# A two-layer trunk in fp32 on one core: the last four row blocks of layer 1's down projection as Strassen block products, and the second feed-forward group's weights prepared before the first group is evacuated

## The chip, the core and the metric

The kernel runs on one core of a Trainium2 chip. A core has five engines, each with its own list of instructions that it works through in order: TensorE (PE in the profile; PEld is its loading of weights), VectorE (DVE), ScalarE (ACT), GpSimd (POOL) and SyncE (SP, which here only issues DMAs). They meet through semaphores. The metric is the time of one execution in microseconds (us) on the device; less is better.

## The reference

Input x is 512 tokens by 1024, in fp32. Two layers follow, each with a mixer and a gated feed-forward part, then a last RMS norm:

```python
def gated_conv_ffn(x, w_gate, w_up, conv_w, conv_b, w_down):
    g = jnp.einsum('bsd,df->bsf', x, w_gate)            # 1024 -> 2816
    g = causal_dwconv3(g, conv_w) + conv_b
    up = jnp.einsum('bsd,df->bsf', x, w_up)             # 1024 -> 2816
    return jnp.einsum('bsf,fd->bsd', jax.nn.silu(g) * up, w_down)   # 2816 -> 1024

for layer in range(2):
    xn = rms_norm(h, norm_mix[layer])
    h = h + mixer(xn)          # layer 0: gated conv and pooling; layer 1: chunked spatial gating
    hn = rms_norm(h, norm_ffn[layer])
    h = h + gated_conv_ffn(hn, ...)
return rms_norm(h, final_norm)
```

## The kernel before

**Precision.** Every fp32 matrix is split into a high and a low part (`whi`/`wlo` for weights, `a_hi`/`a_lo` and `hgh`/`hgl` for activations), and a product is three matmuls: high by high, high by low, low by high (`mm3`, lines 154 to 156; `multiply`, line 543). There are two ways to make the parts of a weight tile. `parts` (L146) copies the high part on ScalarE (L149) and subtracts on VectorE (L150). `summed` (L136) writes the negated high part into `lo` on ScalarE (L140), has a GpSimd DMA add the raw weights to it (L141), and copies the high part (L143).

**Feed-forward.** The 2816 hidden columns are 22 row blocks of 128. They are worked in groups of two blocks: group 0 directly (`direct`), groups 2, 4, ..., 20 in `both` by Strassen's scheme (seven products instead of eight) for gate and up together, 14 products of twelve matmuls of 256 columns. `both(f)` first fetches and combines the weights: the unit a11, the sums s12 and s34 for gate and up (L691 to 719), then runs the products and evacuates them: ScalarE copies banks out (L733), VectorE adds and applies the convolution taps (`conv`, L575 and L577), ScalarE the SiLU (L585). Group 0 is evacuated by the function that `direct` returns (L619 to 631): VectorE scales the gate banks (L624), taps, SiLU, multiplication with the up banks (L630). There are seven PSUM banks for all this.

**Down projection.** `steps` runs the groups in the order of STEPS; after a group comes a part of the down projection of earlier blocks (`half_down`, in layer 1 four row blocks for one half of the 1024 columns). What is left at the end is `last_down` for blocks 18 to 21: eight pieces of 128 tokens by 512 columns, each twelve matmuls (the last piece in two halves of 256 columns). `done` adds a piece to the residual y (L1100), sums its squares (L1145), multiplies by the final gain into `yf` (L1148) and, when a row of 1024 is complete, takes the root (L1158), finishes the norm on VectorE in the columns up to 672 (L1163) and on ScalarE in the rest (L1167), and stores (L1168, L1169). Before it, `root` (L1122) is a one-element square root of a constant that is ready at the very start.

**Order.** A scheduler puts each engine's instructions into a fixed order when the kernel is built, from the order in which the code emits them and what they depend on; `behind` and `inorder` pin a few. Tiles come from pools with a set number of buffers (`raw` 4, `whi` and `wlo` 6 each, `sum` 3, `c` 2); an instruction that writes a tile waits until the buffer's last user is done. Each engine then keeps its order: what stands behind a waiting instruction waits too.

Of the kernel before, what the change touches and what calls it, by code (L numbers as in the profile page):

```python
# [8 lines left out]
F32 = mybir.dt.float32  # L9
# [3 lines left out]
ALU = mybir.AluOpType  # L13
PSUM = bass.MemoryType.PSUM

P = 128
# [16 lines left out]
def tile_trunk(ctx: ExitStack, tc: tile.TileContext, x, norm_mix, norm_ffn, final_norm,  # L33
# [520 lines left out]
    class Ffn:  # L554
# [127 lines left out]
        def both(self, f):  # L682
# [12 lines left out]
            for key in "gu":  # L695
# [23 lines left out]
                put(key, 3, w, 1)  # L719

            banks = {"g": {}, "u": {}}
# [44 lines left out]
        def hidden(self, f, before=lambda i, j: None):  # L766

            if f == 0:
# [11 lines left out]
                rows = rest()  # L780
            else:
                rows = self.both(f)
            return rows
# [293 lines left out]
    def ffn1(norm):  # L1077
        with tc.tile_pool(name="f1", bufs=1) as ap:
# [39 lines left out]
            def last_down(a, b):  # L1118
                fin = wp.tile([P, D], F32, tag="raw", bufs=4, name="fin")
                nc.scalar.dma_start(  # L1120
                    fin, final_norm.rearrange("(o d) -> o d", o=1).to_broadcast([P, D]))
# [7 lines left out]
                def lhs(ft, piece):  # L1129
                    ts_ = slice(piece[0] * P, (piece[0] + 1) * P)  # L1130
                    return acts[ft][0][:, ts_], acts[ft][1][:, ts_]

                def rhs(ft, piece):
                    c = slice(*piece[1:])
                    return ch[ft][0][:, 0, c], ch[ft][1][:, 0, c]

                yf = {}

                def done(piece, ps):
                    t, c0, c1 = piece  # L1140
                    dst = y[t][:, c0:c1]
                    add(dst, ps, t)
                    sq = tp.tile([P, S], F32, tag="sq", name=f"sqf{t}_{c0}")[:, : c1 - c0]
                    ss = ssf[:, t, c0 // 256 : c0 // 256 + 1]
                    nc.scalar.activation(sq, dst, AF.Square, accum_out=ss)  # L1145
                    if c0 == 0:
                        yf["row"] = ap.tile([P, D], F32, tag="sum", bufs=3, name=f"yf{t}")
                    nc.vector.tensor_tensor(yf["row"][:, c0:c1], dst, fin[:, c0:c1], ALU.mult)  # L1148
                    ms = ssf[:, t, 0:1]
                    if c0 == 0:  # L1150
                        nc.vector.tensor_scalar(ss, ss, 1.0 / D, EPS, op0=ALU.mult, op1=ALU.add)
                        return
                    nc.vector.scalar_tensor_tensor(ms, ss, 1.0 / D, ms, op0=ALU.mult, op1=ALU.add)
                    if c1 < D:
                        return
                    r = tp.tile([P, LINE], F32, tag="rc", name=f"rc_fin{t}")[:, :1]
                    sd = work("sd", 1, f"fin{t}")
                    nc.scalar.activation(sd, ms, AF.Sqrt)  # L1158
                    nc.vector.reciprocal(r, sd)
                    nc.vector.scalar_tensor_tensor(ms, ms, r, r, op0=ALU.mult, op1=ALU.mult)  # L1160
                    nc.vector.tensor_scalar(ms, ms, -0.5, 1.5, op0=ALU.mult, op1=ALU.add)
                    lo, hi = slice(0, SHARE), slice(SHARE, D)
                    nc.vector.tensor_scalar(y[t][:, lo], yf["row"][:, lo], r, ms, op0=ALU.mult,  # L1163
                                            op1=ALU.mult)
                    both = ssf[:, t, 1:2]
# [55 lines left out]
```

## Time and profile before

| | us |
|---|---|
| median of 3 runs (991.19 to 992.14) | 991.21 |
| the profiled execution | 991.47 |
| its span | 989.4 |
| TensorE busy | 978.7 |
| VectorE busy | 770.3 |
| ScalarE busy | 549.6 |
| GpSimd busy | 101.0 |

TensorE's clock was granted at full speed throughout (0.999). A row of the timeline has the start in us, the duration in us, the engine, the line, the operation, the tiles written and read, and in brackets how long the engine stood idle before it and what ended that. A row for a stretch has its bounds, its length, then for PE, PEld, DVE, ACT and POOL the busy time and the number of instructions, the granted clock, the DMA engines' share and GB/s. A row of waits has who waited for whom, the total in us, how often, and the longest. A row of DMA issues ends with the median us from issue to landing.

### The profile page before, as it was taken

How to read it: one execution, taken by the hardware profiler on the slowest of the kernel's cores; microseconds unless marked ns; L12 is line 12 of the kernel's file. 1: busy time of each engine (PE TensorE's matmuls, PEld its weight loads, DVE VectorE, ACT ScalarE, POOL GpSimd, SP SyncE). 2: the span in 40 equal slices, each digit the busy share in tenths (PEclk: the TensorE clock that was granted, in tenths of full speed). 3: DMA queues.
4: the chain of work that ended last, by engine and by line, in shares of the span. 5: the costliest groups of instructions: out<-in, count | busy, mean ns of one | idle time of the engine just before them, and what ended most of it. 6: DMA issues, size and time to landing. Idle time of an engine off the chain costs nothing.

```text
span 989.4 us, 15461 instructions
## 1 busy us (share of the span) xinstructions
PE 978.7 (99%) x6117; PEld 882.7 (89%) x6117; DVE 770.3 (78%) x1170; ACT 549.6 (56%) x823; POOL 101.0 (10%) x118
## 2 busy tenths in 40 slices
PE   9999999999999999999999999999999999999997
PEld 6788888899999999999889988889999999999986
DVE  5897458998788887886887665589987779777776
ACT  5623346765465654655487734676655456554544
POOL 2142022100000000000210001210000000000000
PEclk9999999999999999999999999999999999999999
DMA  7342225555455454553324623265555555455512
GB/s 247 131 149 85 86 86 128 131 143 153 129 149 133 131 142 129 150 129 110 124 64 116 199 74 102 54 139 129 150 162 134 131 148 146 118 136 135 143 49 85
DMA packets 86420, 125.64 MB, mean 127 GB/s; under 512 B 4196, under 2 KB 58188, under 8 KB 86348
## 3 DMA queue, kind: packets, MB, share of 16 engines
q1 hardware_dynamic: 77228, 98.24, 32.1%
q0 software_dynamic: 7200, 24.12, 13.4%
q10 hardware_dynamic: 1920, 2.30, 0.8%
q8 instruction: 48, 0.79, 0.3%
q14 instruction: 24, 0.20, 0.1%
HBM read 98.42 MB, written 2.10 MB: 102 GB/s over the span
## 4 chain that ended last, share of the span: by engine, by line
PE 85%; DVE 6%; ACT 3%; issue 1%; DMA 0%; ACTq 0%; POOL 0%; DVEq 0%
PE dn L154 4%; PE dn L155 4%; PE dn L156 4%; PE d L155 3%; PE d L154 3%; PE d L156 3%; PE oo L156 1%; PE oo L154 1%; PE oo L155 1%; PE oe L156 1%; PE oe L155 1%; PE oe L154 1%; PE u_20a L543 1%; PE u_18a L543 1%; PE u_16a L543 1%
## 5 line engine op out<-in xcount | busy, mean ns | idle before, releaser
L154 PE MATMUL dn<-whi_dn,a_hi 128*128 128x512 f32 (+1 forms) x180 | 69.3, 385 | 0.0
L155 PE MATMUL dn<-wlo_dn,a_hi 128*128 128x512 f32 (+1 forms) x180 | 69.3, 385 | 0.0
L156 PE MATMUL dn<-whi_dn,a_lo 128*128 128x512 f32 (+1 forms) x180 | 69.2, 384 | 0.0
L577 DVE SCALAR_TENSOR_TENSOR c<-rows,prm,c 128x512 f32<-128x512 f32 x88 | 63.8, 746 | 0.2 <-ACT c L575 0.2
L141 POOL DMA_DIRECT2D wlo_g<-raw_g x20 | 17.2, 861 | 385.2 <-ACT wlo_g L140 369.6
L154 PE MATMUL d<-a_hi,whi_d 128*128 128x512 f32 x144 | 56.1, 390 | 0.0
L155 PE MATMUL d<-a_lo,whi_d 128*128 128x512 f32 x144 | 56.1, 390 | 0.0
L156 PE MATMUL d<-a_hi,wlo_d 128*128 128x512 f32 x144 | 56.0, 389 | 0.0
L150 DVE TENSOR_TENSOR wlo_dn<-raw_dn,whi_dn 128x1024 fp32r<-128x1024 f32 x22 | 26.9, 1224 | 26.2 <-ACT whi_dn L149 26.0
L680 DVE TENSOR_TENSOR wlo_s34u<-s34u,whi_s34u 128x1024 fp32r<-128x1024 f32 x20 | 24.5, 1225 | 26.7 <-ACT whi_s34u L679 26.7
L1100 DVE SCALAR_TENSOR_TENSOR y<-dn,small,y 128x512 f32<-128x512 f32 (+1 forms) x49 | 33.9, 737 | 8.8 <-PE dn L156 8.8
L156 PEld LDWEIGHTS dn<-whi_dn,a_lo 128*128 128x128 f32 x180 | 33.8, 188 | 6.9 <-DVE a_lo L263 0.2
L154 PEld LDWEIGHTS dn<-whi_dn,a_hi 128*128 128x128 f32 x180 | 33.9, 188 | 6.5
L155 PEld LDWEIGHTS dn<-wlo_dn,a_hi 128*128 128x128 f32 x180 | 33.9, 188 | 6.3
L143 ACT ACTIVATE whi_u<-raw_u 128x1024 fp32r<-128x1024 f32 x21 | 22.1, 1055 | 30.0 <-PE d L155 16.3
L149 ACT ACTIVATE whi_dn<-raw_dn 128x1024 fp32r<-128x1024 f32 x22 | 23.3, 1059 | 25.5 <-issue 12.6
L261 ACT ACTIVATE a_hi<-s 128x512 fp32r<-128x512 f32 x44 | 27.4, 625 | 18.0 <-PE dn L155 12.3
L150 DVE TENSOR_TENSOR wlo_d<-raw_d,whi_d 128x1024 fp32r<-128x1024 f32 x18 | 22.0, 1224 | 19.7 <-ACT whi_d L149 19.7
L199 ACT ACTIVATE hgh<-h,prm 128x512 fp32r<-128x512 f32 x24 | 17.3, 723 | 35.1 <-DVE h L310 35.0
L585 ACT ACTIVATE s<-c,prm 128x512 f32<-128x512 f32 x44 | 31.2, 714 | 9.3 <-DVE c L577 9.3
L141 POOL DMA_DIRECT2D wlo_u<-raw_u x21 | 18.1, 862 | 166.4 <-ACT wlo_u L140 83.8
L210 POOL TENSOR_TENSOR ssq_f<-ssq_f,sq_f 128x512 f32<-128x512 f32 x14 | 19.8, 1412 | 131.2 <-ACT sq_f L209 96.3
(1435 smaller groups left out, 3664.0 us busy)
## 6 DMA issues: line engine op xcount, KB each, us to landing
raw_g<-in_w_ffn_gate_dram SPq DMA_DIRECT2D x40, 512.0 KB, 3.9
raw_u<-in_w_ffn_up_dram SPq DMA_DIRECT2D x40, 512.0 KB, 3.7
raw_dn<-in_w_ffn_down_dram SPq DMA_DIRECT2D x22, 512.0 KB, 3.6
wlo_u<-raw_u POOLq DMA_DIRECT2D x21, 512.0 KB, 5.6
wlo_g<-raw_g POOLq DMA_DIRECT2D x20, 512.0 KB, 4.7
raw_d<-in_w_ffn_down_dram SPq DMA_DIRECT2D x18, 512.0 KB, 3.7
raw_oe<-in_w_out_even_dram SPq DMA_DIRECT2D x8, 512.0 KB, 3.6
raw_v<-in_w_in_odd_dram SPq DMA_DIRECT2D x8, 512.0 KB, 4.6
```

The source lines that it names most:

```text
L141: nc.gpsimd.dma_start(lo, raw, accum_op=ALU.add)
L149: behind(nc.scalar.activation(hi, raw, AF.Copy), after[1])
L150: behind(nc.vector.tensor_tensor(lo, raw, hi.bitcast(F32), ALU.subtract), after[0])
L154: nc.tensor.matmul(ps, lhs[0], rhs[0], start=start, stop=False)
L155: nc.tensor.matmul(ps, lhs[0], rhs[1], start=False, stop=False)
L156: nc.tensor.matmul(ps, lhs[1], rhs[0], start=False, stop=stop)
L261: nc.scalar.activation(hi, src, AF.Copy, scale=scale)
L543: nc.tensor.matmul(ps, l, r, start=first, stop=end, skip_group_check=True)
L577: nc.vector.scalar_tensor_tensor(c, t[:, i : S + i], prm("cf", i * NF + ft), c, op0=ALU.mult, op1=ALU.add)
L585: nc.scalar.activation(s, c, AF.Silu, bias=self.prm("bf", ft))
L680: nc.vector.tensor_tensor(lo, src, hi.bitcast(F32), ALU.subtract)
L1100: nc.vector.scalar_tensor_tensor(dst, ps, ffn.cols[:, t : t + 1], dst, op0=ALU.mult, op1=ALU.add)
```

## The change

**Group 2.** `both` is cut in two, `prepare` (fetch and combine weights) and `products`. In group 0, `prepare(2)` is now called before the returned evacuation `rest()`, so group 2's weights are emitted ahead of it. This is in both layers.

**The last part of layer 1's down projection.** Blocks 18 to 21 (two by two) times 1024 columns (two halves) for 512 tokens (two halves) become seven Strassen products, each for two token tiles. The four weight blocks are fetched and combined by four subtractions (`less`), and all seven weight operands are split by `summed`, so their low parts come by GpSimd's DMA instead of VectorE. The activations are combined on VectorE and split into the tiles of `hg` (`block`) instead of being split row by row. Products accumulate in shared banks, each partial sum being added to y as it stands (`add`); `finish` does what `done` did, with the gain multiplication on GpSimd for the first two token tiles. `fin` moves from the `raw` pool to `sum`, the finished rows from `sum` to `raw`. The one-element square root `root` is gone.

```diff
-        def both(self, f):
+        def prepare(self, f):
...
+            return stat
+
+        def products(self, f, stat):
...
-                rows = rest()
-            else:
-                rows = self.both(f)
-            return rows
+                self.second = self.prepare(2)
+                return rest()
+            return self.products(f, self.second if f == 2 else self.prepare(f))
...
-            def last_down(a, b):
-                fin = wp.tile([P, D], F32, tag="raw", bufs=4, name="fin")
...
-                root = small[:, 2:3]
-                nc.scalar.activation(root, eps, AF.Sqrt)
-                ch = {}
-                for ft in range(a, b):
-                    ch[ft] = weights(w_ffn_down[1][ft * P : (ft + 1) * P, :]
-                                     .rearrange("(k p) c -> p k c", p=P), 1, D, f"dn1_{ft}")
...
+            def finish(t, c0, c1, ssums={}):
+                dst = y[t][:, c0:c1]
+                sq = tp.tile([P, S], F32, tag="sq", name=f"sqf{t}_{c0}")[:, : c1 - c0]
+                ss = ssf[:, t, c0 // 256 : c0 // 256 + 1]
+                nc.scalar.activation(sq, dst, AF.Square, accum_out=ss)
+                if t not in ssums:
+                    row = wp.tile([P, D], F32, tag="raw", bufs=4, name=f"yf{t}")
+                    ssums[t] = [ss, row, 0]
+                ms, row, seen = ssums[t]
+                times = nc.gpsimd if t < 2 else nc.vector
+                times.tensor_tensor(row[:, c0:c1], dst, fin[:, c0:c1], ALU.mult)
...
+                share = SHARE if t == NT - 1 else S
+                lo, hi = slice(0, share), slice(share, D)
...
+            a = NF - 4
+            rows = {ft: row for ft, row in ffn.steps(half_down, before)}
+            raw = {(i, j): fetch(
...
+                for i, j in ((0, 0), (0, 1), (1, 1), (1, 0))}
+            fin = ap.tile([P, D], F32, tag="sum", bufs=3, name="fin")
...
+            less(t1, b12, b11)
+            put(1, summed, b11)
+            put(2, summed, b21)
+            less(t2, b22, t1)
+            put(5, summed, t1)
+            put(6, summed, t2)
+            less(b12, b22, b12)
+            put(3, summed, b22)
+            put(7, summed, b12)
+            less(b21, b21, t2)
+            put(4, summed, b21)
...
+            block(1, 0, a11)
+            block(2, 1, a12)
+            for n in range(2):
+                nc.vector.tensor_tensor(s1[:, n], a21[n], a22[n], ALU.add)
+            block(5, 4, s1)
+            for n in range(2):
+                nc.vector.tensor_tensor(s2[:, n], s1[:, n], a11[n], ALU.subtract)
+            block(6, 5, s2)
+            for n in range(2):
+                nc.vector.tensor_tensor(a12[n], a12[n], s2[:, n], ALU.subtract)
+            block(3, 6, a12)
+            for n in range(2):
+                nc.vector.tensor_tensor(a21[n], a11[n], a21[n], ALU.subtract)
+            block(7, 2, a21)
+            block(4, 3, a22)
...
+            for i in range(2):
+                add(y[i][:, left], product(1, i), i)
+            for i in range(2):
+                add(y[i][:, left], product(2, i), i)
+                finish(i, 0, 512)
+            for i in range(2):
+                add(y[2 + i][:, right], product(5, i), 2 + i)
+            for i in range(2):
+                add(y[i][:, right], product(6, i), i)
+            for i in range(2):
+                add(y[i][:, right], product(3, i), i)
+                finish(i, 512, D)
+            for i in range(2):
+                add(y[2 + i][:, right], product(7, i), 2 + i)
+                finish(2 + i, 512, D)
+
+            add(y[3][:, 256:512], banks["a", 1][:, 256:512], 3)
+            for i, c0, c1, bank in ((0, 0, 512, None), (1, 0, 256, None), (1, 256, 512, "c")):
+                add(y[2 + i][:, c0:c1], product(4, i, c0, c1, bank), 2 + i)
+                finish(2 + i, c0, c1)
```

`put` calls `summed` for a product's weight operand; `product(p, i, ...)` issues the twelve matmuls' half of a product, six for token tile i of 128 rows, with the weights as the moving side. The product 4 of the second tile is done in two pieces of 256 columns.

More of the change, by code (lines that the diff above doesn't have):

```diff
@@ new lines, in ffn1, with put, less @@
+            b11, b12, b21, b22 = (raw[at][0] for at in ((0, 0), (0, 1), (1, 0), (1, 1)))
+            t1, t2 = (ap.tile([P, 2, S], F32, tag="sum", bufs=3, name=f"dnt{i}") for i in (1, 2))
+            stat = {}
+            def put(product, how, src):
+                stat[product] = how(src, 2, 512, f"dnp{product}")
+            def less(dst, x, y_):
+                behind(nc.vector.tensor_tensor(dst, x, y_, ALU.subtract), ffn.added["u"])
+            less(t1, b12, b11)
+            put(1, summed, b11)
@@ new lines, in ffn1 @@
+            left, right = slice(0, 512), slice(512, D)
+            for i in range(2):
[10 more added lines that the diff above has]
+                finish(i, 512, D)
```

104 lines of the change are left out of this document (53 added, 51 removed).

## The prediction

> **What bounds the kernel now.** I read the page's busy shares first, then TensorE's waits, then the stretches where it waited, then the first 40 us and the end by engine.
>
> ```profile
> PE 978.7 (99%) x6117; PEld 882.7 (89%) x6117; DVE 770.3 (78%) x1170; ACT 549.6 (56%) x823; POOL 101.0 (10%) x118
> ...
> q0 software_dynamic: 7200, 24.12, 13.4%
> ...
> wlo_u<-raw_u POOLq DMA_DIRECT2D x21, 512.0 KB, 5.6
> ```
>
> ```profile
> PE u_2e L543 <- DVE wlo_s12u L680: 1.9, 2, 0.9
> ...
> PE g_2a L543 <- ACT rows L733: 0.2, 1, 0.2
> ```
>
> TensorE is the bound: what is taken from its list is worth its own time, unless another engine is then last. It stands still only in group 2 of each layer, at the start, and at the end. The next view is busy time in the two stretches from the first product of group 2 to the first matmul of the down projection.
>
> ```profile
> 169.69:191.46 21.77, 20.66 (x169) 20.25 (x168) 20.64 (x33) 16.94 (x26) 1.71 (x2) 1.00 0.47 124
> 659.06:680.67 21.61, 20.70 (x170) 20.31 (x169) 19.34 (x30) 17.03 (x26) 1.72 (x2) 1.00 0.47 129
> ```
>
> A product takes 1.44 us everywhere in the chain that ended last, so 14 of them are 20.16 us: group 2 loses 1.61 us in layer 0 and 1.45 in layer 1. VectorE's timeline shows why: the up weights' low part stands behind the four conv taps of the evacuation.
>
> ```profile
> 658.87 1.28 DVE L624 TENSOR_TENSOR rows<-gu,rstd_f 128x512 f32<-128x512 f32 x2
> ...
> 660.75 2.74 DVE L577 SCALAR_TENSOR_TENSOR c<-rows,prm,c 128x512 f32<-128x512 f32 x4
> 663.40 1.22 DVE L680 TENSOR_TENSOR wlo_s12u<-s12u,whi_s12u 128x1024 fp32r<-128x1024 f32 x1
> ```
>
> At the start ScalarE feeds TensorE with no slack (whi_ac ends at 34.02, the first matmul that uses it starts at 34.08):
>
> ```profile
> 31.55 0.59 ACT L437 COPY z<-z 128x512 f32<-128x512 f32 x1
> 32.87 0.21 ACT L241 ACTIVATE sd_m0c<-ms_m0c 128x4 f32<-128x4 f32 x1 [0.73 <-DVE ms_m0c L249]
> 32.98 1.04 ACT L149 ACTIVATE whi_ac<-raw_ac 128x1024 fp32r<-128x1024 f32 x1
> ...
> 646.89 1.28 ACT L241 ACT_TABLE_LOAD   x1
> ```
>
> And the end: TensorE's last matmul starts at 982.07 and ends at 982.35; the last square root follows 1.5 us later, the last store 2.29 us after that, and the span ends 3.26 us after the store's issue.
>
> ```profile
> 983.85 0.20 ACT L1158 ACTIVATE sd_fin<-ssf 128x1 f32<-128x1 f32 x1 [0.23 <-DVE ssf L1153]
> 985.52 0.59 ACT L1167 ACTIVATE y<-yf,ssf 128x352 f32<-128x352 f32 x1 [1.47 <-DVE ssf L1166]
> 986.14 0.34 ACTq L1169 DMA_DIRECT2D out_dram<-y  x1
> ```
>
> The profiled execution took 991.47 us (span 989.4 and 2.07 around it), 0.26 above the median of 991.21. A difference within 0.2% (1.98 us) is about what a measurement of this kernel can't tell from none. All clock times below are in the span of before.
>
> **Group 2's weights first.** In the order as built, wlo_s12u comes right behind the two L624 in both layers: in layer 1 it ends at about 661.3, and the fifth product needs it at 659.06 + 4 x 1.44 = 664.8. Late next is the sixth product, which goes into a bank that ScalarE (L733) must first copy out. That copy now stands behind the s12u high part, the two passes over the up weights and two first taps: 659.04 + 3 x 0.95 + 2 x 0.61 + 0.37 = 663.5, due at 659.06 + 3 x 1.44 = 663.4, so about 0.1 late in layer 1; in layer 0 the same sum gives 173.83, due 174.01. What moves back is the evacuation: its taps, its activation table and SiLUs by about 1.5 us, so L630 frees the third bank at about 667.6; the ninth product needs it at 659.06 + 8 x 1.44 = 670.6. The four weight fetches keep their places in SP's list, and POOL's too is unchanged there; only the L141 transfer of the up weights is issued some 1.5 us sooner (landing 666.6 by the 5.6 us row, due 670.6). Gain: 1.55 + 1.3 = 2.85 us; ends 0 (another wait takes its place) and 3.06 (all of it).
>
> **The square root's table.** The removed `root` (L1122) had ScalarE load the table that holds Sqrt at 1.47 us, before there was work. Without it, one more load stands between the third copy of z and the first square root: 31.55 + 0.59 + 0.02 = 32.16, plus 1.28 is 33.44, so the root comes at 33.46 instead of 32.87, and behind it in the queue whi_ac ends at 34.6 instead of 34.02. TensorE's wait for wlo_ac at 35.73 held a slack of 0.16 for this. Cost 0.4; ends 0.3 and 0.6. The Trainium skill ("ScalarE: Activation LUTs", section "What ACT_TABLE_LOAD costs") puts a switch of sets at 1.28 us for the load and 1.38 for a drain; here the trace differs, the load of 646.89 begins 0.02 after the instruction ahead has ended and the next begins 0.02 after it. By that page the sum below would come to -0.1 in place of -1.5.
>
> **The last part: TensorE.** Before: 84 matmuls of 512 columns at 0.2265 and 24 of 256 at 0.12 (starts in the timeline), 21.9 us. After: seven products for each of two token tiles, 78 and 12, 19.1 us: 2.8 less. The second half of layer 1's other down part ends at 949.49 + 48 x 0.2265 = 960.36 as before; without waits the last matmul then ends at 979.4 instead of 982.35.
>
> **Its inputs.** The weights' four subtractions (L150) become four differences of the same 1.13 us on VectorE; the low parts become a negated copy on ScalarE (0.95 more each) and seven transfers from GpSimd. Activations: ten halves at 0.335, two pairs at 0.60 and eight sums at 0.335 in place of four at 0.60, so about 4.8 us more on VectorE. By my working through the queues, VectorE has done this at 965.3. TensorE's dates are 960.4 (product 1, made from rows 18 and 19, long ready), 963.0 (product 2, ready 959.5), 965.7, 968.4, 971.1, 973.9 and 976.6. ScalarE's negated copies start at 945.4, 948, 951, 953, 955.5, then 960.5 and 963.2 (the last two wait for buffers that matmuls free, and the high halves for product 3 stand behind them, at 965.1, needed at 971.1). Each transfer is issued as its copy ends, 1.1 us later, and lands some 5.6 us after that, 6 us or more before use. One of VectorE's differences (b21 less t2) overwrites what the second transfer reads: VectorE stands still from 953.2 until it lands at about 955, and the activation sums queue behind. That uses up slack only: a landing of up to about 7.3 us changes nothing, and each us beyond is a us lost. Cost taken 0.
>
> **Its end.** In the order as built VectorE must, from the end of the first tile's product 7 (960.36 + 66 x 0.2265 + 0.16 = 975.5), do without a break: three adds of 512 (0.66) and three of 256 (0.40), three multiplications by the final gain at 0.60 and two at 0.335, three scalings of 512 columns (0.42 each, estimated from the 672-column one's 0.55), and some twenty one-column operations at 0.08. That is 8.5 us, to 984.0: VectorE, not TensorE, is last, 4.6 us after the last matmul. Then in ScalarE's list the third tile's second half (0.71, estimated from 0.59 for 352 columns) stands ahead of the last square root, which so comes at 984.8 instead of 983.85. From there the chain is the old one: 0.95 us later than before. So the 2.8 us of TensorE aren't cashed. Ends: -2.95 (root 1.5 us after TensorE as before, at 980.9) and +2 more (next paragraph).
>
> Four of the eight multiplications by the gain go to GpSimd. Such an operation holds up VectorE operations that read SBUF alone:
>
> ```profile
> 635.72 1.39 POOL L210 TENSOR_TENSOR ssq_f<-ssq_f,sq_f 128x512 f32<-128x512 f32 x1 [2.57 <-ACT sq_f L209]
> ...
> 635.88 1.52 DVE L644 TENSOR_TENSOR t<-t 128x256 f32<-128x256 f32 x1
> ```
>
> (0.42 otherwise.) Adds that read PSUM ran beside it at their 0.68. By my dates the four run at 968.1 to 970.8 and 973.5 to 976.2, beside adds from PSUM, with the first multiplication of VectorE's own at 976.2: 0 taken, up to 1 us each for the last two if they slip.
>
> **Sum.** -2.85 + 0.4 + 0.95 = -1.5: 991.47 - 1.5 = 990.0 for the profiled execution, 989.7 against the median.
>
> **Rivals.** *The matmuls' saving comes through* (faster): VectorE keeps pace and the last root follows TensorE by 1.5 us: -2.85 + 0.4 - 2.95 = -5.4, 985.8. For it: TensorE bounds everywhere else, VectorE is at 78%. Against: VectorE's list above; parts of it are possible. Chance 0.13.
>
> *The wait in group 2 only changes its name*: the products then stand for ScalarE's copies (margin 0.2 and -0.1) or a freed bank, and nothing is gained: +0.4 + 0.95 = 1.35, 992.6. For it: ScalarE was busy 17 of 21 us there. Against: each later date has about 0.4 us or more. Chance 0.13.
>
> *The table costs twice*: if a load held ScalarE for 2 x 1.28 and more before the next instruction, 1.4 us would be added: -0.1, 991.1. Against: the 0.02 us on both sides of the load in the row above. Chance 0.02.
>
> *The low parts land late* (slower): q0 moved 46 such transfers in 13.4% of 989.4 us, 2.9 us of all engines each; the second to fifth are issued 1.9 to 3.1 us apart. If they share the engines so that the second lands after 4 x 2.9 = 11.6 us, VectorE's wait adds 11.6 - 7.3 = 4.3: 994.0. It decides from a landing of 8.8 us (no gain left). Against: issue to landing was 4.5 to 8.3 in the tile's view. Chance 0.14, with all else that makes it slower.
>
> **Numbers.** My case has 0.58, at 989.7, by itself 988.5 to 991; below 989.23 (0.2%) lies a third of it. Faster by over 0.2%: 0.13 + 0.19 = 0.32. Slower by over 0.2% (993.2): 0.14. Same: 0.54. The range 987.0 to 992.9 leaves out most of the first and third rival, and holds the others.
>
> **What would show it.** Group 2 stretches of 20.2 to 20.4 us and no TensorE wait for wlo_s12u; a table load at 32.2 and the first ac matmul 0.5 late; last matmul 2.8 earlier relative to the other down part; VectorE without idle in the last 8 us and the last root some 5 us behind TensorE. Wrong would make me: TensorE waits in the last part, a first product late, or VectorE idle at the end.

## The result, and the profile after

The changed kernel takes 989.85 us (median; 989.22 to 990.53) against 991.44 (990.95 to 992.44) for the kernel before on the same chip: ratio 0.9983, 95% interval 0.9976 to 0.9989, or -1.6 us [-2.4, -1.1]. The prediction was 989.7, with a range from 987.0 to 992.9. The profiled execution took 989.89, with a span of 988.2 and 1.69 around it (before: 991.47, 989.4 and 2.07).

TensorE's waits in the changed kernel (who waited for whom, us in total, times, longest):

```profile
PE ac L154 <- ACT whi_ac L149: 0.4, 1, 0.4
...
PE u_4e L543 <- DVE wlo_s12u L680: 0.3, 1, 0.3
```

The 1.9 us for wlo_s12u in group 2 are gone. A wait for a tensor of the same name has come up in the next group (u_4e is group 4), and one at ac, at the start.

Busy time of the changed kernel in three stretches, from the first product to the down projection behind it: group 2 of layer 0, group 2 of layer 1, group 4 of layer 0 (bounds, length, then busy time and number of instructions of PE, PEld, DVE, ACT and POOL):

```profile
169.76:189.96 20.20, 20.20 (x170) 20.19 (x168) 19.20 (x31) 16.04 (x25) 1.71 (x2) 1.00 0.50 131
658.09:678.49 20.40, 20.40 (x169) 20.21 (x168) 18.91 (x30) 16.38 (x25) 1.72 (x2) 1.00 0.50 136
195.43:216.14 20.71, 20.40 (x170) 20.20 (x168) 19.42 (x32) 12.10 (x20) 0.85 (x1) 1.00 0.54 154
```

Group 4 of layer 0 in the kernel before:

```profile
196.93:217.08 20.15, 20.15 (x169) 20.15 (x168) 18.59 (x30) 11.69 (x20) 0.85 (x1) 1.00 0.53 149
```

So group 2 went from 21.77 to 20.20 and from 21.61 to 20.40, and group 4 of layer 0 from 20.15 to 20.71.

The start and the end of the changed kernel in its timeline (start, duration, engine, line, operation, idle time before):

```profile
31.36 0.58 ACT L437 COPY z<-z 128x512 f32<-128x512 f32 x1
31.96 1.28 ACT L241 ACT_TABLE_LOAD   x1
33.25 0.20 ACT L241 ACTIVATE sd_m0c<-ms_m0c 128x4 f32<-128x4 f32 x1
33.37 1.04 ACT L149 ACTIVATE whi_ac<-raw_ac 128x1024 fp32r<-128x1024 f32 x1
...
34.46 0.50 PE L154 MATMUL ac<-hgh,whi_ac 128*128 128x512 f32 x1 [0.42 <-ACT whi_ac L149]
...
977.04 0.28 PE L1234 MATMUL dn_c<-whi_dnp,hgl 128*128 128x256 f32 x1
...
982.01 0.72 ACT L1151 ACTIVATE y<-yf,ssf 128x512 f32<-128x512 f32 x1 [0.92 <-DVE ssf L1150]
982.64 0.19 ACT L1142 ACTIVATE sd_fin<-ssf 128x1 f32<-128x1 f32 x1
...
984.85 0.34 ACTq L1153 DMA_DIRECT2D out_dram<-y  x1
```

The table's load now stands in the chain, and whi_ac comes late by it. At the end the last matmul ends at 977.32, the last root starts 5.3 us later (before: 1.5), the last store is issued 7.53 us after the last matmul (before: 3.79). ScalarE's scaling of the third tile (L1151) stands directly ahead of that root. The chain that ended last, of the changed kernel, tells who fills that time (start, us, engine, tile, line):

```profile
971.82 1.37 PE dn_a L1234 x6
973.19 0.02 issue
973.22 0.31 DVE y L1103
...
974.03 0.66 DVE yf L1132
974.69 0.66 DVE y L1103
...
977.51 0.66 DVE y L1103
...
979.14 0.60 DVE yf L1132
...
980.15 0.40 DVE y L1103
```

The chain leaves TensorE for good at 973.19, 4.1 us before its last matmul ends, and stays on VectorE until 982. Put together, against the kernel before:

| stage | before | after | difference |
|---|---|---|---|
| up to the first z matmul | 7.32 | 7.13 | -0.19 |
| from there to the first product of group 2 | 162.37 | 162.63 | +0.26 |
| group 2, layer 0 | 21.77 | 20.20 | -1.57 |
| group 4, layer 0 | 20.15 | 20.71 | +0.56 |
| group 2, layer 1 | 21.61 | 20.40 | -1.21 |
| other down part's second half and last part, to the end of the last matmul | 33.02 | 30.17 | -2.85 |
| last matmul's end to the last store's issue | 3.79 | 7.53 | +3.74 |
| last issue to the span's end | 3.26 | 3.35 | +0.09 |

These are -1.17; all other stages differ by 0.03 together, and the spans, which are printed to 0.1 us, by -1.2. Another 0.38 lies outside the span. A second profiled execution of the changed kernel, taken for the last experiment, has the same stages from the first z matmul on (162.61, 20.16, 20.71, 20.39, 30.17 and 7.53), but its first z matmul is at 7.33: the -0.19 in the first row does not belong to the change.

### The profile page after: what moved, and what is told of

The parts are those of the page before. It is cut to its first block, busy times and chain, and to the rows that moved or that the text cites. A ratio compares the mean times of both kernels' runs of the same rounds, so it can differ in the third digit from the quotient of the medians.

```text
span 988.2 us, 15489 instructions
## 1 busy us (share of the span) xinstructions
PE 974.7 (99%) x6099; PEld 880.1 (89%) x6099; DVE 775.0 (78%) x1189; ACT 560.6 (57%) x841; POOL 111.0 (11%) x129
## 4 chain that ended last, share of the span: by engine, by line
PE 85%; DVE 7%; ACT 2%; issue 1%; DMA 0%; POOL 0%; ACTq 0%; DVEq 0%
PE dn L154 3%; PE dn L155 3%; PE dn L156 3%; PE d L155 3%; PE d L154 3%; PE d L156 3%; PE oo L156 1%; PE oo L154 1%; PE oo L155 1%; PE oe L156 1%; PE oe L154 1%; PE oe L155 1%; PE u_20a L543 1%; PE u_18a L543 1%; PE u_16a L543 1%
## 5 line engine op out<-in xcount | busy, mean ns | idle before, releaser
L154 PE MATMUL dn<-whi_dn,a_hi 128*128 128x512 f32 x144 | 56.2, 390 | 0.0
L155 PE MATMUL dn<-wlo_dn,a_hi 128*128 128x512 f32 x144 | 56.1, 390 | 0.0
L156 PE MATMUL dn<-whi_dn,a_lo 128*128 128x512 f32 x144 | 56.0, 389 | 0.0
L150 DVE TENSOR_TENSOR wlo_dn<-raw_dn,whi_dn 128x1024 fp32r<-128x1024 f32 x18 | 22.0, 1224 | 23.6 <-ACT whi_dn L149 23.4
L261 ACT ACTIVATE a_hi<-s 128x512 fp32r<-128x512 f32 x40 | 25.0, 626 | 15.7 <-PE dn L155 9.9
L200 DVE SCALAR_TENSOR_TENSOR hgl<-h,prm,hgh 128x512 fp32r<-128x512 f32 x24 | 23.1, 964 | 12.0 <-ACT hgh L199 11.9
L156 PEld LDWEIGHTS dn<-whi_dn,a_lo 128*128 128x128 f32 x144 | 27.0, 188 | 5.7
L156 PEld LDWEIGHTS d<-a_hi,wlo_d 128*128 128x128 f32 x144 | 27.0, 188 | 5.6
L1103 DVE SCALAR_TENSOR_TENSOR y<-dn,small,y 128x512 f32<-128x512 f32 x40 | 27.6, 743 | 5.6 <-PE dn L156 5.6
L154 PEld LDWEIGHTS dn<-whi_dn,a_hi 128*128 128x128 f32 x144 | 27.1, 188 | 5.4
```

The lines of the kernel that those rows point to most:

```text
L150: behind(nc.vector.tensor_tensor(lo, raw, hi.bitcast(F32), ALU.subtract), after[0])
L154: nc.tensor.matmul(ps, lhs[0], rhs[0], start=start, stop=False)
L155: nc.tensor.matmul(ps, lhs[0], rhs[1], start=False, stop=False)
L156: nc.tensor.matmul(ps, lhs[1], rhs[0], start=False, stop=stop)
L200: nc.vector.scalar_tensor_tensor(hg[k][1], h[k], g, hg[k][0].bitcast(F32), op0=ALU.mult, op1=ALU.subtract)
L261: nc.scalar.activation(hi, src, AF.Copy, scale=scale)
```

## Experiments

The theory: group 2's weights first are the whole gain, less what group 4 of layer 0 gives back; the block products save TensorE 2.85 us, which VectorE, last in the end, eats and more. The rivals: the wait in group 2 has only been renamed and the gain is the matmuls'; the missing early root costs nothing or much; the low parts' DMAs cost.

**Group 2's weights first, alone** (kernel before; old last part, early root kept):

```diff
-        def both(self, f):
+        def prepare(self, f):
...
+                self.second = self.prepare(2)
+                return rest()
```

> The kernel before with one part of the change alone: group 2's weights are prepared ahead of the first evacuation; the old last part and the early square root stay. Theory (the gain sits in group 2): by the traces of before and after, TensorE gets through group 2 of layer 0 in 20.2 us instead of 21.77 (-1.57) and of layer 1 in 20.4 instead of 21.61 (-1.21), and gives back 0.56 in group 4 of layer 0, where a weight's low part is late on VectorE: -2.2 us against before, ratio 0.9978. The load of the square root's table stays at the start and the first ac matmul is not late. Rival (the gain of the whole change comes from its last part, the wait in group 2 only changes its name): 0, ratio 1.0. A second rival (the 0.56 in group 4 belongs to the missing early square root and not to this part): -2.8, ratio 0.9972.

Measured: 988.74 against 991.37, ratio 0.9971 [0.9959, 0.9982], or -2.6 us by the medians; as a median more than the whole change gains. The three stretches of this kernel, in the same order:

```profile
169.47:189.63 20.16, 20.16 (x170) 20.15 (x168) 19.15 (x31) 16.01 (x25) 1.71 (x2) 1.00 0.49 131
658.27:678.67 20.40, 20.40 (x169) 20.19 (x168) 18.91 (x30) 16.38 (x25) 1.72 (x2) 1.00 0.50 137
195.09:215.78 20.69, 20.40 (x169) 20.19 (x168) 19.40 (x32) 12.04 (x20) 0.85 (x1) 1.00 0.56 153
```

-1.61, -1.21 and +0.54: the gain is there without the block products, so the first rival falls. The second gave the time that was measured, but the interval holds the theory's as well, and by the stages it falls too: the loss in group 4 is there with the early root in its place.

**The block products, alone** (changed kernel, group 2's weights back behind the evacuation, early root kept):

```diff
-                self.second = self.prepare(2)
                 return rest()
-            return self.products(f, self.second if f == 2 else self.prepare(f))
+            return self.products(f, self.prepare(f))
...
+            root = small[:, 2:3]
+            nc.scalar.activation(root, eps, AF.Sqrt)
```

> The changed kernel with group 2's weights put back behind the evacuation and with the early square root: only the last part in block products is left of the change. Theory (TensorE's 2.85 us are not cashed because VectorE is last): the last matmul ends 2.85 us sooner, the last store is issued 7.5 us after it instead of 3.8, so +0.9 us against before, ratio 1.0009. Rival (the matmuls' saving comes through): -2.9, ratio 0.9971. Rival (the last part neither gains nor loses): 0.

Measured: 992.89 against 991.37, ratio 1.0012 [1.0003, 1.0021]. The end of this kernel in its timeline:

```profile
979.74 0.28 PE L1235 MATMUL dn_c<-whi_dnp,hgl 128*128 128x256 f32 x1
...
985.33 0.19 ACT L1141 ACTIVATE sd_fin<-ssf 128x1 f32<-128x1 f32 x1
...
987.54 0.34 ACTq L1152 DMA_DIRECT2D out_dram<-y  x1
```

The last root is 5.3 us behind the last matmul's end (980.02) and the last issue 7.52, the same as in the full change. The last part in seven products is slower than the old one with eight: by 0.12% in the times, and by 0.9 us in the stage (37.70 us to the last issue, 36.81 before).

**Five more matmuls ahead of the last product** (changed kernel):

```diff
+            spare = aux_bank("spare")
+            for _ in range(5):
+                nc.tensor.matmul(spare, blocks[7][0][:, 0, :P], stat[7][0][:, 0, :], start=True,
+                                 stop=True)
             add(y[3][:, 256:512], banks["a", 1][:, 256:512], 3)
```

> The changed kernel with five more matmuls of 512 columns (5 x 0.2265 = 1.13 us), of which nothing is used, ahead of the last product. Theory (VectorE is last by a wide margin): product 4's first bank is then complete at 977.0 and VectorE comes to it at 977.4; the last bank at 978.5 and VectorE comes to it at 980.1: 0 against after (ratio to before 0.998), last store's issue unmoved, and VectorE without a new wait. Rival (TensorE sets the end): +1.13, ratio 0.9995.

Measured: 990.04 against 991.37, ratio 0.9987 [0.9979, 0.9996]; after's 0.9983 lies inside. The times alone leave room for half a us; the trace does not. From the first matmul of the other down part's second half (948.88 here, 947.15 in after) the last matmul ends after 31.31 us instead of 30.17, and the last store is issued after 37.69 instead of 37.70. TensorE has over 1.1 us to spare there.

**The early square root back** (changed kernel):

```diff
+            root = small[:, 2:3]
+            nc.scalar.activation(root, eps, AF.Sqrt)
             a = NF - 4
```

> The changed kernel with the early one-element square root put back, nothing else. Theory by the two traces: its absence moved TensorE from the second half of the first mixer product on by 0.27 us, so -0.27 against after (ratio to before some 0.9981 where after has 0.9983). The prediction's own figure: -0.4. Rival (the load is paid somewhere else once it is at the start): 0. Rival (the load's full 1.28 us was lost): -1.28, ratio 0.9971. The load is seen near 1.5 us, none at 32, and the first ac matmul stands 0.04 to 0.1 us after whi_ac's end without having waited.

Measured: 990.03 against 991.37, ratio 0.9985 [0.9977, 0.9994]: no difference from after that the times could show. In its trace the load stands where it costs nothing:

```profile
1.47 1.28 ACT L1158 ACT_TABLE_LOAD   x1 [1.47 <-PEq L1283]
...
34.10 0.50 PE L154 MATMUL ac<-hgh,whi_ac 128*128 128x512 f32 x1
```

From the first z matmul (7.31) to the first product of group 2 (169.70) it takes 162.39 us, 0.24 less than after. The theory's 0.27 is met in this stage; the profiled execution lost it again in a wait at another place (u_0a, 0.3 us, further down).

**Group 4's low part by DMA** (changed kernel, layer 0, group 4, up weights only):

```diff
                 def split_s12():
-                    self.halves(*w, s12)
+                    if (layer, f, key) != (0, 4, "u"):
+                        return self.halves(*w, s12)
+                    nc.scalar.activation(w[1], s12, AF.Copy, scale=-1.0)
+                    nc.gpsimd.dma_start(w[1], s12, accum_op=ALU.add)
+                    nc.scalar.activation(w[0], s12, AF.Copy)
```

> The changed kernel with one low part moved: in group 4 of layer 0 the up weights' s12 sum gets its low part by a negated copy on ScalarE and a GpSimd DMA instead of a subtraction at the end of VectorE's backlog (wlo_s12u, 201.23 to 202.43 in after, wanted at 201.18). Theory (the first group 2's gain of 1.57 us is given back in part because VectorE works without a break from 178 to 203 and that low part comes 0.3 to 0.56 us late): group 4 of layer 0 takes 20.15 us from its first product to the down projection instead of 20.71, TensorE's wait for wlo_s12u is gone, and the time is 0.56 less than after's (989.3 by after's median). Rival (the next low part in VectorE's list is late instead, or ScalarE's extra 0.95 us delays a bank's copy): the group still takes 20.5 us or more, 0.

Measured: 991.23 against 991.89, ratio 0.9996 [0.9987, 1.0005]: by the medians 1.4 us slower than after, though the two intervals just touch. Its stage says the same: group 4 took 22.08 us instead of 20.71. The timeline of ScalarE and GpSimd in this kernel:

```profile
191.29 1.04 ACT L709 ACTIVATE whi_s12u<-s12u 128x1024 fp32r<-128x1024 f32 x1
...
197.82 1.05 ACT L707 ACTIVATE wlo_s12u<-s12u 128x1024 fp32r<-128x1024 f32 x1
...
199.16 0.85 POOL L708 DMA_DIRECT2D wlo_s12u<-s12u  x1 [3.50 <-ACT wlo_s12u L707]
```

The high part is copied at 191.29, the negated copy only at 197.82, behind the bank copies, SiLUs and rows that the order put ahead of it. The DMA then needed 5.0 us, and TensorE waited 1.5 us. The rival had the group at 20.5 us or more, which came, but not for its reasons: the expectation took VectorE's list as the only place where this operand could be late.

**Group 4's weights ahead of the rows' splitting** (on the kernel with group 2's weights first alone, old last part):

```diff
                 if part is not None:
                     half_down(*part)
+                if f == 2 and 4 in self.early:
+                    self.second = self.prepare(4)
                 if ready:
                     self.split_acts(rows)
```

> The kernel before with group 2's weights first (the run that had only this), and layer 0's group 4 weights prepared ahead of the splitting of group 2's rows, so that wlo_s12u of group 4 stands ahead of the two L263 subtractions on VectorE instead of behind them. Theory (in layer 0 VectorE's order, not its amount of work alone, gives 0.55 us back): wlo_s12u then ends 1.2 us sooner, at about 201.2 in after's clock, just when it is wanted; group 4 takes 20.15 us instead of 20.69 and the time is 0.5 less than the run with group 2's weights alone (988.2, ratio to before 0.9965). Rival (what is moved back, the rows' low parts or the s34u low part, is then late): group 4 or the down part behind it loses the same 0.5, 988.7.

Measured: 988.88 against 991.38, ratio 0.9978 [0.9969, 0.9987]. The times do not tell it from the run without it (0.9971 [0.9959, 0.9982]); its stretch does:

```profile
195.10:215.25 20.15, 20.15 (x169) 20.14 (x168) 19.79 (x33) 12.09 (x20) 0.85 (x1) 1.00 0.53 151
```

20.15 instead of 20.69, with VectorE even busier: it was the order of VectorE's list that had cost the 0.55. The rival, by which as much is lost behind group 4, falls by the trace: from there to group 2 of layer 1 it takes 442.2 us, against 442.5 without this step. Its span was 986.5 against 987.4; 0.4 of that is a wait at u_0a that this execution did not have (see the end).

**Low parts of the last part on VectorE** (changed kernel):

```diff
-                stat[product] = how(src, 2, 512, f"dnp{product}")
+                stat[product] = parts(src, 2, 512, f"dnp{product}")
```

> The changed kernel with the seven weight operands of the last part split in the old way, the low parts by subtraction on VectorE instead of ScalarE copy and GpSimd DMA. VectorE gets 7 x 1.13 = 7.9 us more; in after it stood idle between 944 and 974 for 1.0 (its wait for the second transfer, which goes) + 0.5 + 3 x 0.6 + 0.5 = 3.9 us. Theory (VectorE is the bound of the last 40 us): +4.0 against after, 993.9, with TensorE waiting for late low parts. Rival (the low parts on VectorE fit into its idle time): 0. Rival (the transfers and the wait they bring cost more than they save): -1.

Measured: 996.17 against 991.89, ratio 1.0042 [1.0030, 1.0055]. TensorE's waits of this kernel that after does not have:

```profile
PE dn_c L1234 <- DVE hgl L1199: 1.6, 1, 1.6
...
PE dn_b L1234 <- DVE hgl L1199: 1.0, 1, 1.0
PE dn_a L1234 <- DVE y L1103: 0.4, 1, 0.4
```

From the other down part's second half to the last issue it takes 42.49 us instead of 37.70: +4.8, where 4.0 was expected. The medians differ by 6; the profiled execution (995.09) was the fastest of the five, and what the others had more is not shown. VectorE is the bound of this stage; without the seven DMAs the block products would cost that much more.

**Fewer passes of VectorE at the end** (changed kernel):

```diff
-                times = nc.gpsimd if t < 2 else nc.vector
-                times.tensor_tensor(row[:, c0:c1], dst, fin[:, c0:c1], ALU.mult)
+                if t < 2 or c0 == 512:
+                    times = nc.gpsimd if t < 2 else nc.vector
+                    times.tensor_tensor(row[:, c0:c1], dst, fin[:, c0:c1], ALU.mult)
...
+                    nc.vector.scalar_tensor_tensor(y[t][:, lo], y[t][:, lo], both, fin[:, lo],
+                                                   op0=ALU.mult, op1=ALU.mult)
```

> The changed kernel with less work on VectorE at the end: for token tiles 2 and 3 the first 512 columns aren't multiplied by the gain on the way, but in the last scaling (one operation of two factors), the common factor is formed first, and ScalarE takes 512 columns of the last tile instead of 352. Theory (VectorE's list sets the end): three multiplications (0.68 + 0.42 + 0.42) leave the list ahead of the last square root and 0.2 comes back, so the last root comes 1.2 us sooner after the last matmul (4.1 instead of 5.3), and the stores 0.45 sooner after the root since ScalarE no longer waits for VectorE's pass: -1.7 against after, 988.2. Rival (ScalarE's list or the last add sets the last root): only the 0.45, 989.4. Rival (TensorE sets the end): 0.

Measured: 989.92 against 991.89, ratio 0.9982 [0.9973, 0.9991]: as after. The end of this kernel in its timeline:

```profile
981.84 0.75 DVE L1153 SCALAR_TENSOR_TENSOR y<-y,ssf,fin 128x512 f32<-128x512 f32 x1
982.51 0.15 DVE L1138 SCALAR_TENSOR_TENSOR ssf<-ssf 128x1 f32<-128x1 f32 x1
...
981.84 0.72 ACT L1155 ACTIVATE y<-yf,ssf 128x512 f32<-128x512 f32 x1
982.59 0.37 ACTq L1157 DMA_DIRECT2D out_dram<-y  x1
983.01 0.20 ACT L1143 ACTIVATE sd_fin<-ssf 128x1 f32<-128x1 f32 x1 [0.45 <-DVE ssf L1138]
...
984.83 0.37 ACTq L1157 DMA_DIRECT2D out_dram<-y  x1
```

The last root comes 4.8 us after the last matmul's end (978.21) instead of 5.3, the last issue 6.6 instead of 7.5: 0.9 of the expected 1.7. The rest was lost to order, on two engines. On VectorE tile 2's scaling (0.75) stands ahead of the last tile's one-column sum, which so ends at 982.66. On ScalarE tile 2's scaling and the issue of its store, until 982.96, stand ahead of the last root. The root before it came 0.03 us behind its sum (980.74, 980.77) and the last one 0.35 behind, so here ScalarE's list came last, by 0.3: for that part the first rival holds. And of the 0.9, 0.6 came back behind the issue: the span ended 3.97 us after it, not 3.35, with the last tile's two stores of 256 KB each issued together. Taking work from VectorE was not enough.

**A new end** (changed kernel, with the early root and group 4's weights ahead; the last part's finish rewritten):

```diff
+            def scale_hi(t, root=None):
...
+                behind(nc.scalar.activation(y[t][:, hi], row[:, hi], AF.Copy, scale=both), root)
...
+                add(y[2 + i][:, right], product(7, i), 2 + i)
+                sums(2 + i, 512, D, nc.gpsimd)
...
+            root_of(2)
+            last = root_of(3)
+            scale_hi(1, last)
+            scale_hi(2)
+            scale_lo(2)
+            scale_hi(3)
+            scale_lo(3, 256)
```

> The changed kernel with the early square root, group 4's weights ahead as in the other run of this call, and a new division of the end: the gain multiplications of token tiles 2 and 3 in columns 512 to 1023 go to GpSimd, those of columns 0 to 511 into the last scaling; the table for the square root is loaded by a one-element root when ScalarE has nothing to do (after product 2); both last roots stand ahead of any last scaling of the tiles 1 to 3 on ScalarE, and the last tile's sum ahead of VectorE's scaling of tile 2; the last tile is scaled and stored in two pieces of 256 columns on VectorE and 512 on ScalarE. Theory (VectorE's list at the end, in its amount and its order, is what eats TensorE's 2.85 us): VectorE's full-width work from 973.2 on is six adds (3.2 us), two scalings of 0.46, one of 0.67 and two of 0.4, and its last one ends at about 981.1 in after's clock, so the last store is issued at 981.3 instead of 984.85 and 4.0 us after the last matmul instead of 7.5; with 0.3 us more for the larger last stores -3.2, with the early root -0.27 and group 4 -0.55: 985.8, ratio to before 0.9945. Rival (the end is set by the last matmul's own chain or by ScalarE, which has 6 to 7 us of work there): no less than 6 us from the last matmul to the last issue, 987.5 or more. Rival (GpSimd's two more multiplications hold up VectorE's scalings by up to 1.3 us): 987.

Measured: 989.37 against 991.38, ratio 0.9982 [0.9973, 0.9991], where 985.8 was expected. VectorE and GpSimd in the timeline of this kernel:

```profile
970.79 4.02 POOL L1136 TENSOR_TENSOR yf<-y,fin 128x512 f32<-128x512 f32 x3 [3.51 <-DVE y L1106]
...
973.54 1.28 DVE L1148 SCALAR_TENSOR_TENSOR ssf<-ssf,rc_fin 128x1 f32<-128x1 f32 x1
...
976.00 1.28 POOL L1136 TENSOR_TENSOR yf<-y,fin 128x512 f32<-128x512 f32 x1 [1.19 <-DVE rc_fin L1147]
...
976.30 0.99 DVE L1148 SCALAR_TENSOR_TENSOR ssf<-ssf,rc_fin 128x1 f32<-128x1 f32 x1
```

An operation on one column, 0.21 us in after, took 1.28 and 0.99, and both times ended when GpSimd's multiplication did (974.81 and 977.28). In consequence TensorE waited 0.8 us for a bank that VectorE had not yet added to y. The second rival named GpSimd as the cause, but had the full-width scalings held up, not these. The last issue came 36.40 us after the other down part's second half began (after: 37.70), and the span ended 4.28 us after that.

**The new end, with VectorE's small operations reading one tensor**:

```diff
-                nc.vector.scalar_tensor_tensor(ms, ms, r, r, op0=ALU.mult, op1=ALU.mult)
+                nc.vector.tensor_scalar(ms, ms, r, r, op0=ALU.mult, op1=ALU.mult)
...
+            scale_hi(1)
+            scale_lo(1)
             add(y[3][:, :256], product(4, 1, 0, 256), 3)
```

> The run with the new end, with two edits: VectorE's one-column operations of two SBUF tensors (the Newton step, the sum of squares, the common factor) are written as operations of one tensor with per-row factors, and tile 1 is scaled and stored before the last tile's adds instead of behind the last root. In the run with the new end two such operations of one column took 1.28 and 0.99 us (0.21 in after) and ended with GpSimd's multiplications at 974.8 and 977.3; TensorE then waited 0.8 for a bank. Theory (a GpSimd multiplication holds up VectorE operations that read two SBUF tensors, however small, and not those that read one): no one-column operation takes over 0.3 us, TensorE has no wait in the last part, the last store is issued some 4.0 us after the last matmul, 1.9 us sooner than in the run with the new end, and fewer stores are under way at the end: 987.3. Rival (the hold is for every VectorE operation on SBUF, one tensor too): the same one or two us are lost again, 989.0 to 989.4. Rival (the last stores' landing takes what is won, 4.3 us in the run with the new end): 988.3.

Measured: 989.34 against 991.44, ratio 0.9980 [0.9971, 0.9989]. VectorE and GpSimd in the timeline of this kernel:

```profile
974.66 1.29 POOL L1136 TENSOR_TENSOR yf<-y,fin 128x512 f32<-128x512 f32 x1 [0.23 <-DVE rc_fin L1147]
...
974.96 0.27 DVE L1148 TENSOR_SCALAR ssf<-ssf,rc_fin 128x1 f32<-128x1 f32 x1
...
975.14 1.10 DVE L1165 TENSOR_SCALAR y<-yf,ssf 128x512 f32<-128x512 f32 x1
...
977.46 0.47 DVE L1165 TENSOR_SCALAR y<-yf,ssf 128x512 f32<-128x512 f32 x1
```

The small operations are free now (0.15 to 0.27) and TensorE does not wait in the last part, so that half of the theory holds. But a scaling of 512 columns, one tensor in, took 1.10 beside GpSimd's multiplication and 0.47 without it, so "only operations that read two tensors" was wrong. The last issue came 6.3 us after the last matmul, not 4.0: behind the late scaling stood the last tile's sums, and ScalarE's last square waited 0.32 us for VectorE to have added the sum before it. The time is that of the rival by which every VectorE operation on SBUF is held, but its ground is not: small ones of one tensor were not. The landing rival's part came out as well: the span ended 4.27 us after the last issue, with a megabyte of stores issued within 1.3 us.

**The fastest version and the changed kernel side by side**, on one chip:

> The changed kernel once more, unaltered, on the same chip as the next run: 989.9, ratio to before 0.9983.

> The old last part with group 2's weights first and layer 0's group 4 weights ahead, once more, on the same chip as the changed kernel. Theory (the block products of the last part cost what VectorE and the stores do after them, about 0.9 us, the missing early square root 0.27 and the late low part in group 4 0.55): 1.5 us or so less than the changed kernel of this call, 988.4 to 988.9. Rival (the last part in block products costs nothing): no more than 0.8 less.

Measured: the changed kernel 989.89 (ratio 0.9981 [0.9972, 0.9990]); the old last part with group 2's weights first and group 4's ahead 988.26 (0.9963 [0.9950, 0.9975]), 1.63 us less than the changed kernel and 3.5 less than the kernel before. This version beats both.

The ends of these kernels in one table, in us from the first matmul of the other down part's second half (the last column to 0.1 us, as the span is printed):

| kernel | last matmul ends | last issue | span ends |
|---|---|---|---|
| before | 33.02 | 36.81 | 40.07 |
| weights first alone | 33.01 | 36.80 | 40.07 |
| changed kernel | 30.17 | 37.70 | 41.05 |
| block products alone | 30.18 | 37.70 | 41.06 |
| five more matmuls | 31.31 | 37.69 | 41.02 |
| low parts on VectorE | 34.48 | 42.49 | 45.78 |
| fewer passes | 30.18 | 36.80 | 40.77 |
| new end | 31.28 | 36.40 | 40.68 |
| new end, one-tensor operations | 30.20 | 36.50 | 40.77 |

No version of the block products' end came below the old one's 40.07.

## Why the prediction was right

**Group 2's weights first** (-2.85 predicted): -1.57 and -1.21 are -2.78. The stretches came out at 20.20 and 20.40, inside the 20.2 to 20.4 given, and the 0.24 left over in layer 1 is at gate's product 6, the fourth in order: it starts 1.59 us after the one ahead instead of 1.44, and the next one 1.54 after it. The prediction had it 0.1 late there. The rival that the wait only changes its name falls for group 2. What the prediction missed is one step further: it asked what is late next inside group 2, not in the groups after it. VectorE ran without a break from 178 to 203 in layer 0. Its list reached the low part for group 4's fifth product 0.2 us sooner than before (201.44 then), while TensorE came to that product 1.5 us sooner, at 201.18 (202.68 before, when the low part had just been finished, at 202.66): +0.56. This is the step that the prediction left out. The two rows that show it, from VectorE's timeline of the changed kernel:

```profile
200.02 1.27 DVE L263 TENSOR_TENSOR a_lo<-s,a_hi 128x512 fp32r<-128x512 f32 x2
201.23 1.20 DVE L680 TENSOR_TENSOR wlo_s12u<-s12u,whi_s12u 128x1024 fp32r<-128x1024 f32 x1
```

**The square root's table** (+0.4 predicted): +0.26 by the stages of after, +0.24 by the run with the root back. The load came at 31.96 and took 1.28, and the first ac matmul was 0.57 late relative to the first z matmul (34.46 - 7.13 against 34.08 - 7.32), as said. The term was mis-sized because 0.3 of that delay had been made up by 37.3, where the prediction let only 0.16 be. The 0.16 is the wait for wlo_ac, which is gone. Nearly all of the rest is that TensorE no longer stops there: the three wlo_ac matmuls behind the wait took 0.81 us to the next one in the kernel before (35.73 to 36.54) and take 0.69 without it (35.95 to 36.64).

The Trainium skill ("ScalarE: Activation LUTs", "What ACT_TABLE_LOAD costs") counts a drain of 1.38 us beside the load. The trace differs again: the load starts 0.02 after the copy ends, the root 0.01 after the load.

**The last part on TensorE** (-2.8 predicted): -2.85, and no wait. **Its inputs** (0): VectorE stood 1.03 us for the second transfer, and went on 4.9 us after its issue (947.16, 952.04), under the 7.3 from which it would have cost. The profile names no releaser for this wait; that it is the transfer is read from the code and from the run with the low parts on VectorE, where the wait is gone. The rival of late low parts falls, and the run with the low parts on VectorE shows what they are worth: 4.8 us.

**Its end** (+0.95 net of TensorE's saving predicted): -2.85 + 3.74 + 0.09 = +0.98. VectorE was without idle time of note from 973.22 to 981.9, and the last root came 5.3 us behind TensorE ("some 5"). ScalarE's part in it came as predicted too: VectorE's last sum ended at 982.04, but the third tile's scaling (982.01, 0.72 us) still stood ahead of the root at 982.64. The rival that the matmuls' saving comes through falls three times: by the block products alone (+0.12%), by the five matmuls that cost nothing, and by the chain that leaves TensorE at 973.19. GpSimd's multiplications cost 0 in the changed kernel, as taken: VectorE's first multiplication starts at 974.00, 0.02 us after GpSimd's last one ends, and the two one-column sums of two tensors that fell beside them (972.53 and 973.88) began 0.1 us before an end (972.62 and 973.98). The prediction had the first from its dates; that one-column operations can be held up too it did not know, and that they were not is luck.

**The sum.** -2.78 + 0.26 + 0.98 = -1.54 for the steps that were predicted (-1.5). The missed +0.56 was met by two things that the prediction did not contain: -0.19 before the first z matmul, ahead of all that the change touches, and -0.38 outside the span. So the total's agreement to 0.2 us is partly luck: these two made up for the one that was missed. Two of its readings were off without effect: a product does not take 1.44 us everywhere in the chain (two in group 2 of layer 1 take 1.58 and 1.60), and the other down part's second half begins at 949.33, not 949.49.

## What to carry to other kernels

When a wait on the bounding engine is taken away, follow the engine that caused it through the following groups too: if it runs without a break, it takes back what it has not been relieved of, and moving its next due item ahead (here 0.55 us) is a separate step. Work saved on TensorE in the last stage is worth nothing when another engine already finishes later; ask which engine's list the final chain runs through, and how much must be stored after the last reduction, before counting matmuls. A change of several parts should be timed part by part: here one part gained 0.29% by itself and another lost 0.12%.

## What the runs showed of the hardware that was not expected

**A GpSimd multiplication holds VectorE operations of two SBUF tensors, even of one column.** Beside a GpSimd multiplication of 512 columns (1.28 us) a one-column VectorE operation of two SBUF tensors took 1.28 and 0.99 us instead of 0.21; a one-column operation of one tensor took 0.15 to 0.27, as without it; a scaling of 512 columns of one tensor took 1.10 instead of 0.47; adds that read PSUM took their 0.74. The Trainium skill ("SBUF — State Buffer", "Who interferes with whom") names as contending with GpSimd the operations with two SBUF inputs and those single-input ones that run in a mode using both ports. The two-tensor case, the full-width case of one tensor and the adds from PSUM agree with it. The one-column case of one tensor agrees if it runs outside that mode, which no run here shows.

**A landing time decides over a us.** In the second mixer VectorE waits for a weight from DRAM, in every kernel. VectorE's row in the changed kernel:

```profile
526.41 1.23 DVE L919 TENSOR_TENSOR raw_u<-raw_u,raw_u 128x1024 f32<-128x1024 f32 x1 [2.23 <-DMA raw_u<-in_w_in_odd_dram]
```

The same row, and TensorE's wait that follows from it, in the kernel with five more matmuls:

```profile
528.29 1.23 DVE L919 TENSOR_TENSOR raw_u<-raw_u,raw_u 128x1024 f32<-128x1024 f32 x1 [4.10 <-DMA raw_u<-in_w_in_odd_dram]
```

```profile
PE u_0a L543 <- ACT u L941: 1.6, 1, 1.6
```

That wait was 0, 0.3, 0.4 and 1.6 us in different executions, though nothing near it was changed. At its largest it equals the whole effect looked for, and at 0.3 it covers the early root's 0.24 in the profiled execution of the run with that root back. That it differs from execution to execution of one kernel is likely, not shown: of the eleven executions with five more matmuls two took 991.6 and 991.8 and the others 989.8 to 990.3, and only the one at 991.6 has a profile. A wait at the first z matmuls varied in the same way (0 to 1.6). Effects below 0.5 us had to be read from single stages.

**The time outside the span differs by kernel.** It was 1.7 us in every profiled execution with the block products' end, 2.07 in the kernel before, and 1.8 to 1.9 with group 2's weights first and the old end. No run here tells why.

**Stores at the end.** The span ended 3.26 to 3.35 us after the last issue where one tile of 512 KB was left to store behind the last root in two stores issued 0.7 us apart, the smaller one last; 3.97 where the last tile's two stores, of 256 KB each, were issued within 0.02 us; and 4.27 to 4.28 in the new ends, where the second to last tile's stores went out with the last one's. That the amount in flight sets it is argued from these cases; no run changed it alone.
